# Every product matmul walks its columns in pieces of four, with a hop of 64 bytes, in four passes over the row

## The chip, the cores and the metric

The kernel runs on one core of one Trainium2 chip. The metric is the device time of one execution in microseconds (us). Before the change the median of three runs is 770.9 us (770.83 to 771.6).

## What is computed

The reference has one layer (`DEPTH = 1`), and that layer is the gated short-convolution mixer between two RMS norms. Batch is 1, there are 1024 rows (positions), the model width is 1024, the inner width 2048, and the convolution has 3 taps. All data is float32.

```python
def rms_norm(x, g):
    y = x * lax.rsqrt(jnp.mean(x * x, axis=-1, keepdims=True) + EPS)
    return y * g

def short_conv_mixer(u, w_in, conv_w, w_out):
    z, bg, cg, v = jnp.split(u @ w_in, 4, axis=-1)          # w_in: 1024 x 8192
    y = bg * causal_dwconv(cg * v, conv_w) * jax.nn.silu(z)
    return y @ w_out                                        # w_out: 2048 x 1024

u = rms_norm(x, pre_norm)
out = x + rms_norm(short_conv_mixer(u, sc_w_in, sc_conv_w, sc_w_out), post_norm)
```

## The kernel before

Nearly all of the work is two matrix products, and both run on TensorE (PE in the profile). A matmul instruction there holds a stationary operand of 128x128 weights and lets a moving operand of 128 partitions by 512 or 256 columns stream past it; the result, 128 partitions by the same columns, is added into a PSUM bank (512 float32 columns). Each matmul is preceded by its own weight load, which the profile lists as PEld.

**Three matmuls for one product.** The operands are float32, and the fast type on TensorE is float32r, which rounds. So every operand is split into a high part and a low part (`hi`, `lo` of the weights, `UH`, `UL` of the normed input), and a product is three matmuls into the same bank: `lo` x `UH`, `hi` x `UL`, `hi` x `UH`.

**Seven products for eight.** The input product is cut into 2x2 blocks (two halves of the contraction, two halves of 512 rows) and computed with seven block products in place of eight; they are called a to g. There are 16 channel blocks of 128 and two pairs of outputs for each (gate and value, then z and the other gate), so 32 pairs `p`. The banks are `px`, `py` and `pv`. Function `product` issues the twelve matmuls of one block product: four contraction tiles of 128 by three matmuls, 512 columns each. The first pair is computed by eight products (`plain`, banks `pp`). For most channel blocks the products b, f and g are cut once more in the same way: `deep_product` issues matmuls of 256 columns (banks with a 2 in the name, as `px2b`, and also `px`, `pv`). The output product is done in the same fashion by `out_mm` (512 columns, banks `po_x`, `po_v`) and `small_mm` (256 columns, banks `pb_`, `pf_`).

**Where the moving operand lies.** U stands in SBUF tiles of shape [128, 2, 4, 512] (high and low part, four contraction tiles, 512 rows), so the columns of one matmul are 512 or 256 neighbouring float32 in each partition. The output columns are neighbours in the bank as well. All start addresses of U's slices and of the output slices in the built program are multiples of 64 bytes.

**What sets the order.** All instructions are recorded first and then put in an order by a planner (class `Plan`), which knows the number of elements of an operand and which stretch of a tile it touches, but not the order in which an instruction walks it. TensorE's own order is the recorded order. The waits between engines are semaphores, set by the layer that emits the program. The names in the rows below are the program's tiles; a row says operation, out<-moving operand,weights and the shape.

Of the kernel before, what the change touches and what calls it, by code (L numbers as in the profile page):

```python
# [668 lines left out]
def kernel(  # L669
# [16 lines left out]
    nc = plan = Plan(tc.nc)  # L686
# [29 lines left out]
    def bank(name):  # L716
        return psum.tile([P, HB], F32, tag="bank", name=name)
# [136 lines left out]
    UH, UL = {}, {}  # L854
# [7 lines left out]

    banks = {}

    def product(p, i, ks=None):

        w = wt[p, i]
        which = {"b": "y", "e": "v", "f": "v"}.get(i, "x")
        first = i in "abe"
        if first and (p, which) not in banks:  # L870
            banks[p, which] = bank(f"p{which}_{p}")
        ps = banks[p, which]
        for k in range(KH) if ks is None else ks:
            hi, lo = (h[:, k * P : (k + 1) * P] for h in w)
            last = k == KH - 1
            nc.tensor.matmul(ps, lo, UH[i][:, k], start=first and k == 0, stop=False, skip_group_check=True)
            nc.tensor.matmul(ps, hi, UL[i][:, k], start=False, stop=False, skip_group_check=True)
            nc.tensor.matmul(ps, hi, UH[i][:, k], start=False, stop=last, skip_group_check=True)

    sn, cvs = {}, {}  # L880

# [235 lines left out]
    def plain(p, n, half, part, kks=range(4), first=None, last=None):  # L1117

        i = "abef"[2 * half + part]
        if (p, n, half) not in banks:  # L1120
            banks[p, n, half] = bank(f"pp_{p}_{n}_{half}")
        ps, w = banks[p, n, half], plain_w[p, n, part]
        first = part == 0 if first is None else first
        last = part == 1 if last is None else last
        for j, kk in enumerate(kks):
            hi, lo = (h[:, kk * P : (kk + 1) * P] for h in w)
            end = last and j == len(kks) - 1
            nc.tensor.matmul(ps, hi, UH[i][:, kk], start=first and j == 0, stop=False, skip_group_check=True)
            nc.tensor.matmul(ps, lo, UH[i][:, kk], start=False, stop=False, skip_group_check=True)
            nc.tensor.matmul(ps, hi, UL[i][:, kk], start=False, stop=end, skip_group_check=True)  # L1130

    def plain_snap(p, n):
        t = page(f"sp{n}_{p}")
# [69 lines left out]
    for k in range(KH):  # L1203
        plain(0, 0, 0, 0, [k], first=k == 0)
        for t in range(TH - 2 if k < KH - 1 else 0, TH):
            turn(k + KH, t)
# [5 lines left out]
    square_v(TH + 1)  # L1212
    plain_snap(0, 0)
    plain(0, 1, 0, 0)
    for k in (6, 7):
        read_k(k)
    high_plain(0, 1, [1])
    low_plain(0, 1, [1])
    plain_snap(0, 1)
    plain(0, 0, 0, 1)  # L1220
    plain(0, 1, 0, 1)
    rebuild([0])
# [45 lines left out]
    def plain_late(kk, part):  # L1268

        for n in (0, 1):  # L1270
            plain(0, n, 1, part, [kk], first=part == 1 and kk == 0, last=part == 0 and kk == KH - 1)

    product(1, "b", (0, 1))
    turn2(0)
    second(0)
    product(1, "b", (2, 3))
    sn[1, "a"] = page("sna_1")
    nc.scalar.copy(sn[1, "a"], banks[1, "y"])
    product(1, "a", (0, 1))
    turn2(1)  # L1280
    second(1)
# [105 lines left out]
    HH, KQ = HB // 2, KH // 2  # L1387
# [72 lines left out]
    def deep_product(z, c, i):  # L1460


        n, off = DEEP_W[i]
        if z == "f" and i in ("b'", "g'"):
            ps, first = banks[2 * c + (i == "g'"), "v"], False
        elif z == "g" and i in ("b'", "f'", "g'"):
            ps, first = banks[2 * c + (i == "g'"), "x"][:, HH if i == "f'" else 0 :], False
        else:
            which, first = z + DEEP_C[i][0], i in ("a'", "b'", "e'")
            if first:  # L1470
                banks[c, which] = bank(f"p{which[1]}2{z}_{c}")
            ps = banks[c, which]
        ps = ps[:, :HH]
        for k in range(KQ):
            hi, lo = (h[:, off + k * P : off + (k + 1) * P] for h in deep_w[z, c, n])
            if (z, i) in deep:
                uh, ul = (t[:, k] for t in deep[z, i])
            else:
                kk, l0 = {"a'": (k, 0), "b'": (k + KQ, 0), "e'": (k, HH), "f'": (k + KQ, HH)}[i]
                uh, ul = (u[z][:, kk, l0 : l0 + HH] for u in (UH, UL))  # L1480
            nc.tensor.matmul(ps, lo, uh, start=first and k == 0, stop=False, skip_group_check=True)
            nc.tensor.matmul(ps, hi, ul, start=False, stop=False, skip_group_check=True)
            nc.tensor.matmul(ps, hi, uh, start=False, stop=k == KQ - 1, skip_group_check=True)

    def deep_after(c, i):
        which, row, half = DEEP_C[i]
# [190 lines left out]
    for p in range(2, len(PAIRS)):  # L1677
        q, c = p + 1, p // 2
# [91 lines left out]
    for n, slot in enumerate(slots):  # L1770
        if slot[2:]:
            z, i, c = slot
            deep_product(z, c, i)
            if (i, c) == ("e'", LAST[z] - 1) and LAST[z] < NC:
                restore_u(z)

            early = (z, i) in (("f", "c'"), ("f", "e'"))
            if early:
                deep_after_f(c, i)
            if (z, i) != ("f", "c'"):  # L1780
                prepare(n)
            if z == "f":
                if not early:
                    deep_after_f(c, i)
                continue
            if z == "g":
                deep_after_g(c, i)
                if (i, c) == ("d'", NC - 1):
                    at_end("g")
                continue  # L1790
            deep_after(c, i)
            if (i, c) == ("f'", NC - 1):
                third_unit(0)
            elif i == "g'" and c == NC - 1:
                nc.scalar.activation(sn[2 * c + 1, "a"], sn[2 * c + 1, "a"], AF.Silu)
            continue
        i, p = slot
# [89 lines left out]
    def out_mm(i, h, q):  # L1887
        which = "v" if i == "e" else "x"
        if (which, q) not in ob:
            ob[which, q] = bank(f"po_{which}{q}")  # L1890
        ps, u, y = ob[which, q], OP["u", i, h], OP["y", i, h]
        for k in range(CQ):
            hi, lo = (y[:, z, k, q * P : (q + 1) * P] for z in (0, 1))
            first, last = i in "abe" and h == 0 and k == 0, h == 1 and k == CQ - 1
            nc.tensor.matmul(ps, lo, u[:, 0, k], start=first, stop=False, skip_group_check=True)
            nc.tensor.matmul(ps, hi, u[:, 1, k], start=False, stop=False, skip_group_check=True)
            nc.tensor.matmul(ps, hi, u[:, 0, k], start=False, stop=last, skip_group_check=True)

    def halves_of(t):
        q = t % TH  # L1900
# [79 lines left out]
    def small_mm(of_, i):  # L1980
        which = {"b'": "y'", "e'": "v'", "f'": "v'"}.get(i, "x'")
        first = i in ("a'", "b'", "e'")
        if first:
            ob[which] = bank(f"p{of_}_{which[0]}")
        if i in OUT_A:
            n, a0 = OUT_A[i]
            yh, yl = (small_op[of_, n][:, z, :, a0 : a0 + HH] for z in (0, 1))
        else:
            yh, yl = (small_op[of_, "X"][:, 0, z] for z in (0, 1))
        if i in OUT_B:  # L1990
            n, b0 = OUT_B[i]
            uh, ul = (small_op[of_, n][:, z, :, b0 : b0 + HH] for z in (0, 1))
        else:
            uh, ul = (small_op[of_, "X"][:, 1, z] for z in (0, 1))
        for j in (0, 1):
            ps = ob[which][:, j * HH : (j + 1) * HH]
            for k in range(CQ):
                hi, lo = (y[:, k, j * P : (j + 1) * P] for y in (yh, yl))

                start, stop = first and j == 0 and k == 0, k == CQ - 1  # L2000
                nc.tensor.matmul(ps, lo, uh[:, k], start=start, stop=False, skip_group_check=True)
                nc.tensor.matmul(ps, hi, ul[:, k], start=False, stop=False, skip_group_check=True)
                nc.tensor.matmul(ps, hi, uh[:, k], start=False, stop=stop, skip_group_check=True)

    def small_add(of_, i):
        which, row, half = DEEP_C[i]
# [68 lines left out]
    for i, h in OUT[:-2]:  # L2075
        if i in "bf":
            if h == 0:
                product_b() if i == "b" else product_f()
            continue
        for q in range(TH):  # L2080
            out_mm(i, h, q)
        BESIDE[i, h]()
        if h == 1:
            for q in range(TH):
                combine(i, q)
# [5 lines left out]
    for q in range(TH):  # L2091
        for h in (0, 1):
            out_mm("g", h, q)
        if q == TH - 1:
            plan.flush(PLAN)
        combine("g", q)
        finish_row(q + TH)
# [24 lines left out]
```

## Time and profile before

| | |
|---|---|
| median of three runs | 770.9 us (770.83 to 771.6) |
| span of the profiled execution, first to last instruction | 768.7 us |
| its own time outside the profiler | not given; the median stands 2.2 us above the span |
| TensorE busy (matmuls) | 758.4 us, 99% of the span, 4320 instructions |
| weight loads busy (beside the matmuls) | 665.9 us, 4320 instructions |
| VectorE (DVE) busy | 678.9 us, 1022 instructions |
| ScalarE (ACT) busy | 459.4 us, 880 instructions |
| GpSimd (POOL) busy | 464.1 us, 416 instructions |
| granted TensorE clock, mean | 0.998 |

How to read it: matmuls are pipelined, and the profile models the end of each, so a matmul's listed duration (390 ns for 512 columns) is longer than what it adds to the time. What it adds is the distance from its start to the start of the next one. Of the 4320 matmuls 102 are no products: 36 small ones that only keep the clock up (`pw`), 64 transposes of the input (`pk`) and two tiny transposes. The other 4218 are the products: 2244 of 512 columns and 1974 of 256.

### The profile page before, as it was taken

To read this page: it belongs to the slowest core of one execution; us is meant where nothing else is said; L and a number is where in the kernel's file an instruction comes from. 1 tells how busy PE (TensorE), PEld (TensorE's weight loads), DVE (VectorE), ACT (ScalarE), POOL (GpSimd) and SP (SyncE) were. 2 spreads that over 40 slices of the span, in tenths; PEclk is the share of its full clock that TensorE was granted. 3 is DMA by queue.
4 is the path that set the end of the run, shared out by engine and by line. 5 is a ranking of instruction groups with operands and counts; after the bars stand their busy time and mean duration, and the time that the engine had idled before them with its cause. 6 is when DMAs were issued, how large, how long until landed. Compare 5 with 4: busy or idle time off the path is not lost.

```text
span 768.7 us, 12791 instructions
## 1 busy us (share of the span) xinstructions
PE 758.4 (99%) x4320; PEld 665.9 (87%) x4320; DVE 678.9 (88%) x1022; ACT 459.4 (60%) x880; POOL 464.1 (60%) x416
## 2 busy tenths in 40 slices
PE   8999999999999999999999999999999999999996
PEld 6888888898989898988898898989888889889885
DVE  6899978999988979989999999898988898877993
ACT  7765678675656565556555665556553656564731
POOL 2509997889675778696789678584739100600421
PEclk9999999999999999999999999999999999999999
DMA  9213325243333547576859484928465998666842
GB/s 317 68 55 84 110 83 150 103 139 130 98 117 97 171 110 200 136 187 164 252 125 255 103 240 97 255 85 211 122 177 179 334 363 291 203 221 204 278 148 109
DMA packets 117137, 130.11 MB, mean 169 GB/s; under 512 B 7320, under 2 KB 74704, under 8 KB 116944
## 3 DMA queue, kind: packets, MB, share of 16 engines
q1 hardware_dynamic: 112560, 120.77, 49.3%
q0 software_dynamic: 4352, 8.39, 7.2%
q8 instruction: 34, 0.56, 0.3%
q14 instruction: 31, 0.25, 0.1%
q10 hardware_dynamic: 160, 0.14, 0.1%
HBM read 101.74 MB, written 44.30 MB: 190 GB/s over the span
## 4 chain that ended last, share of the span: by engine, by line
PE 97%; DVE 1%; DMA 1%; ACT 0%; POOL 0%; issue 0%; POOLq 0%; ACTq 0%
PE px L292 39%; PE pv L292 15%; PE po_x L292 11%; PE px2b L292 5%; PE px2f L292 4%; PE px2g L292 3%; PE po_v L292 3%; PE pp L292 3%; PE pv2b L292 3%; PE pv2f L292 2%; PE pf_x L292 1%; PE pb_x L292 1%; PE py2b L292 1%; PE py L292 1%; PE pv2g L292 1%; PE pb_v L292 1%
## 5 line engine op out<-in xcount | busy, mean ns | idle before, releaser
L292 PE MATMUL px<-u_a,wah 128*128 128x512 f32 x248 | 76.6, 390 | 0.0
L292 PE MATMUL px<-u_c,wch 128*128 128x512 f32 x248 | 76.5, 390 | 0.0
L292 PE MATMUL px<-u_d,wdh 128*128 128x512 f32 x248 | 76.4, 389 | 0.0
L292 PE MATMUL pv<-u_e,weh 128*128 128x512 f32 x248 | 76.3, 389 | 0.0
L292 ACT COPY beside<-raw 128x512 f32<-128x512 f32 x67 | 39.6, 591 | 31.1 <-DVE wal L292 10.4
L292 DVE SCALAR_TENSOR_TENSOR cv<-gpad,cw,cv 128x1024 f32<-128x1024 f32 x32 | 51.6, 1612 | 3.5 <-ACT cv L292 3.3
L292 PEld LDWEIGHTS px<-u_c,wch 128*128 128x128 f32 x248 | 46.5, 188 | 8.9
L292 PEld LDWEIGHTS px<-u_a,wah 128*128 128x128 f32 x248 | 46.6, 188 | 8.9
L292 PEld LDWEIGHTS pv<-u_e,weh 128*128 128x128 f32 x248 | 46.5, 188 | 8.7
L292 PEld LDWEIGHTS px<-u_d,wdh 128*128 128x128 f32 x248 | 46.6, 188 | 8.6
L292 POOL TENSOR_TENSOR sf<-raw,sc 128x512 f32<-128x512 f32 x30 | 47.2, 1573 | 9.5 <-DVE sc L292 7.1
L292 PE MATMUL px<-u_a,wal 128*128 128x512 f32 x124 | 48.4, 391 | 0.0
L292 PE MATMUL px<-u_c,wcl 128*128 128x512 f32 x124 | 48.4, 391 | 0.0
L292 PE MATMUL px<-u_d,wdl 128*128 128x512 f32 x124 | 48.4, 390 | 0.0
L292 PE MATMUL pv<-u_e,wel 128*128 128x512 f32 x124 | 48.2, 389 | 0.0
L292 POOL TENSOR_TENSOR rs_post<-ve_post,minus_half 128x1 f32<-128x1 f32 x7 | 6.5, 941 | 67.3 <-DVE ve_post L292 67.3
L292 POOL TENSOR_TENSOR sc<-se,raw 128x512 f32<-128x512 f32 x25 | 35.0, 1401 | 19.2 <-DVE se L292 10.2
L292 POOL TENSOR_TENSOR raw<-raw,raw 128x512 f32<-128x512 f32 x31 | 44.6, 1437 | 3.2 <-DVE se L292 2.9
L292 ACT COPY sna<-px 128x512 f32<-128x512 f32 x30 | 17.6, 586 | 45.4 <-PE px L292 45.1
L292 POOL TENSOR_TENSOR se<-raw,raw 128x512 f32<-128x512 f32 x22 | 32.8, 1491 | 18.1 <-DMA raw<-in_sc_w_in 11.3
L292 DVE TENSOR_TENSOR wcl<-sc,wch 128x512 fp32r<-128x512 f32 x31 | 31.7, 1023 | 2.8 <-ACT wch L292 2.8
L292 DVE TENSOR_TENSOR sna<-px2b,sna 128x256 f32<-128x256 f32 x56 | 23.2, 415 | 10.2 <-PE px2b L292 10.2
(486 smaller groups left out, 2637.3 us busy)
## 6 DMA issues: line engine op xcount, KB each, us to landing
raw<-in_sc_w_in SPq DMA_DIRECT2D x128, 256.0 KB, 4.7
y_d<-cv SPq DMA_DIRECT2D x16, 512.0 KB, 2.9
s_d<-s SPq DMA_DIRECT2D x32, 256.0 KB, 4.9
t_d<-in_sc_w_out POOLq DMA_DIRECT2D x16, 512.0 KB, 8.5
tb<-in_sc_w_out SPq DMA_DIRECT2D x16, 256.0 KB, 3.5
t_d<-in_sc_w_out SPq DMA_DIRECT2D x16, 256.0 KB, 4.6
t_d<-t_d SPq DMA_DIRECT2D x16, 256.0 KB, 4.5
s<-y_d SPq DMA_DIRECT2D x16, 256.0 KB, 4.6
```

Source lines behind the costliest of these rows:

```text
L292: getattr(engine, name)(*(self.plain(a) for a in args), **{k: self.plain(a) for k, a in kw.items()})
```

## The change

A helper `walk` gives the same columns in another order, and every product matmul uses it for the moving operand and for the output alike. A row of 512 columns is seen as 32 groups of 16 columns (64 bytes), each group as four pieces of four columns (16 bytes). The instruction takes the first piece of each group, hopping 64 bytes from piece to piece, then the second piece of each, and so on: four passes over the row. With 256 columns there are 16 groups. Each column still meets its own output column once, so the sums are the same. Weights, transposes and warm-up matmuls stay as they are.

```diff
+    def walk(a):
+        return a.rearrange("p (h c n) -> p c h n", c=4, n=4)
+
     def product(p, i, ks=None):
 ...
-            nc.tensor.matmul(ps, lo, UH[i][:, k], start=first and k == 0, stop=False, skip_group_check=True)
-            nc.tensor.matmul(ps, hi, UL[i][:, k], start=False, stop=False, skip_group_check=True)
-            nc.tensor.matmul(ps, hi, UH[i][:, k], start=False, stop=last, skip_group_check=True)
+            nc.tensor.matmul(walk(ps), lo, walk(UH[i][:, k]), start=first and k == 0, stop=False, skip_group_check=True)
+            nc.tensor.matmul(walk(ps), hi, walk(UL[i][:, k]), start=False, stop=False, skip_group_check=True)
+            nc.tensor.matmul(walk(ps), hi, walk(UH[i][:, k]), start=False, stop=last, skip_group_check=True)
 ...
     def out_mm(i, h, q):
 ...
-            nc.tensor.matmul(ps, lo, u[:, 0, k], start=first, stop=False, skip_group_check=True)
+            nc.tensor.matmul(walk(ps), lo, walk(u[:, 0, k]), start=first, stop=False, skip_group_check=True)
 ...
```

The same edit is made to all three matmuls in `plain`, `deep_product`, `out_mm` and `small_mm`.

The order of the instructions is the same on all five engines; only shapes and some waits differ. On TensorE, at the second product of a pair in the middle of the head (`px_668` and `pv_747` are banks, `u_c` and `u_e` moving operands, `wch`, `wcl`, `weh`, `wel` the high and low weights), this stood before:

```order
L292 MATMUL px_668<-u_c,wcl_692 128x512
L292 MATMUL px_668<-u_c,wch_685 128x512 x2
L292 MATMUL pv_747<-u_e,wel_702 128x512 [waits DVE_49]
L292 MATMUL pv_747<-u_e,weh_675 128x512 x2
L292 MATMUL pv_747<-u_e,wel_702 128x512
```

and now:

```order
L292 MATMUL px_668<-u_c,wcl_692 128x4x32x4
L292 MATMUL px_668<-u_c,wch_685 128x4x32x4 x2
L292 MATMUL pv_747<-u_e,wel_702 128x4x32x4 [waits DVE_49,PE_49]
L292 MATMUL pv_747<-u_e,weh_675 128x4x32x4 x2
L292 MATMUL pv_747<-u_e,wel_702 128x4x32x4
```

Nothing moved; the first matmul into a bank that was used before now also waits for TensorE's own semaphore, that is for the matmuls of the bank's earlier use. Such waits stand on 111 instructions of TensorE's queue in place of 62. One of the 62 that were there before, at the start of the pair ahead of that place on TensorE:

```order
L292 MATMUL px_417<-u_g,wgl_609 128x512
L292 MATMUL px_417<-u_g,wgh_608 128x512 x2
L292 MATMUL px_668<-u_a,wal_643 128x512 [waits DVE_49,PE_49]
L292 MATMUL px_668<-u_a,wah_642 128x512 [waits Activation_49]
L292 MATMUL px_668<-u_a,wah_642 128x512
```

This place stands in the new program unchanged but for the shapes.

More of the change, by code (lines that the diff above doesn't have):

```diff
@@ L1127, in plain @@
             end = last and j == len(kks) - 1
-            nc.tensor.matmul(ps, hi, UH[i][:, kk], start=first and j == 0, stop=False, skip_group_check=True)
-            nc.tensor.matmul(ps, lo, UH[i][:, kk], start=False, stop=False, skip_group_check=True)
-            nc.tensor.matmul(ps, hi, UL[i][:, kk], start=False, stop=end, skip_group_check=True)
+            nc.tensor.matmul(walk(ps), hi, walk(UH[i][:, kk]), start=first and j == 0, stop=False, skip_group_check=True)
+            nc.tensor.matmul(walk(ps), lo, walk(UH[i][:, kk]), start=False, stop=False, skip_group_check=True)
+            nc.tensor.matmul(walk(ps), hi, walk(UL[i][:, kk]), start=False, stop=end, skip_group_check=True)
     def plain_snap(p, n):
@@ L1480, in deep_product @@
                 uh, ul = (u[z][:, kk, l0 : l0 + HH] for u in (UH, UL))
-            nc.tensor.matmul(ps, lo, uh, start=first and k == 0, stop=False, skip_group_check=True)
-            nc.tensor.matmul(ps, hi, ul, start=False, stop=False, skip_group_check=True)
-            nc.tensor.matmul(ps, hi, uh, start=False, stop=k == KQ - 1, skip_group_check=True)
+            nc.tensor.matmul(walk(ps), lo, walk(uh), start=first and k == 0, stop=False, skip_group_check=True)
+            nc.tensor.matmul(walk(ps), hi, walk(ul), start=False, stop=False, skip_group_check=True)
+            nc.tensor.matmul(walk(ps), hi, walk(uh), start=False, stop=k == KQ - 1, skip_group_check=True)
     def deep_after(c, i):
@@ L1894, in out_mm @@
             first, last = i in "abe" and h == 0 and k == 0, h == 1 and k == CQ - 1
-            nc.tensor.matmul(ps, lo, u[:, 0, k], start=first, stop=False, skip_group_check=True)
-            nc.tensor.matmul(ps, hi, u[:, 1, k], start=False, stop=False, skip_group_check=True)
-            nc.tensor.matmul(ps, hi, u[:, 0, k], start=False, stop=last, skip_group_check=True)
+            nc.tensor.matmul(walk(ps), lo, walk(u[:, 0, k]), start=first, stop=False, skip_group_check=True)
+            nc.tensor.matmul(walk(ps), hi, walk(u[:, 1, k]), start=False, stop=False, skip_group_check=True)
+            nc.tensor.matmul(walk(ps), hi, walk(u[:, 0, k]), start=False, stop=last, skip_group_check=True)
     def halves_of(t):
@@ L2000, in small_mm @@
                 start, stop = first and j == 0 and k == 0, k == CQ - 1
-                nc.tensor.matmul(ps, lo, uh[:, k], start=start, stop=False, skip_group_check=True)
-                nc.tensor.matmul(ps, hi, ul[:, k], start=False, stop=False, skip_group_check=True)
-                nc.tensor.matmul(ps, hi, uh[:, k], start=False, stop=stop, skip_group_check=True)
+                nc.tensor.matmul(walk(ps), lo, walk(uh[:, k]), start=start, stop=False, skip_group_check=True)
+                nc.tensor.matmul(walk(ps), hi, walk(ul[:, k]), start=False, stop=False, skip_group_check=True)
+                nc.tensor.matmul(walk(ps), hi, walk(uh[:, k]), start=False, stop=stop, skip_group_check=True)
     def small_add(of_, i):
```

## The prediction

> **What bounds the kernel now.** I read the page's busy times first, then the chain that ended last, then the list of waits of TensorE, and last the timeline of TensorE, to get the distance between starts.
>
> ```profile
> span 768.7 us, 12791 instructions
> PE 758.4 (99%) x4320; PEld 665.9 (87%) x4320; DVE 678.9 (88%) x1022; ACT 459.4 (60%) x880; POOL 464.1 (60%) x416
> PEclk9999999999999999999999999999999999999999
> PE 97%; DVE 1%; DMA 1%; ACT 0%; POOL 0%; issue 0%; POOLq 0%; ACTq 0%
> ```
>
> The first row is the span, the second the busy time of each engine, the third the granted TensorE clock in 40 slices (at least nine tenths everywhere), the fourth the chain of waits that ended last. TensorE holds 97% of that chain. It is not late for anything but its own stream:
>
> ```profile
> PE pk L292 <- DVE ve_pre L292: 1.5, 1, 1.5
> PE pw L292 <- DVE idle L292: 1.1, 1, 1.1
> PE pp L292 <- ACT u_a L292: 0.5, 1, 0.5
> PE pk L292 <- DVE xa L292: 0.4, 1, 0.4
> ```
>
> These are all of TensorE's waits in the whole span: 3.5 us, all in the head. So what one product matmul takes, from its start to the next one's start, is the kernel's time. The next rows (start, length, what, count) give it, first for 256 columns and then for 512:
>
> ```profile
> 703.80 2.99 PE L292 MATMUL pf_x<-oB_f,oA_f 128*128 128x256 f32 x24
> 706.63 3.03 PE L292 MATMUL pf_v<-oB_f,oA_f 128*128 128x256 f32 x24
> 709.49 3.03 PE L292 MATMUL pf_x<-oB_f,oA_f 128*128 128x256 f32 x24
> 712.36 2.90 PE L292 MATMUL pf_v<-oB_f,ox_f 128*128 128x256 f32 x24
> 715.10 3.02 PE L292 MATMUL pf_x<-ox_f,oA_f 128*128 128x256 f32 x24
> 717.97 22.00 PE L292 MATMUL po_x<-ou_d,oy_d 128*128 128x512 f32 x96
> 739.80 22.14 PE L292 MATMUL po_x<-ou_g,oy_g 128*128 128x512 f32 x96
> ```
>
> From 703.80 to 717.97 there are five groups of 24, so 14.17 us / 120 = 118.1 ns for a matmul of 256 columns. From 717.97 to 739.80 there are 96, so 21.83 / 96 = 227.4 ns for 512. The 256 further columns cost 109.3 ns: 0.427 ns a column, and 227.4 - 512 x 0.427 = 8.8 ns a matmul whatever its width. The whole stream is 2244 x 227.4 + 1974 x 118.1 ns = 510.3 + 233.1 = 743.4 us, of which the columns (1,654,272 of them) are 706.4 us. The first product starts here:
>
> ```profile
> 12.61 0.50 PE L292 MATMUL pp<-u_a,wn00h 128*128 128x512 f32 x1 [0.45 <-ACT u_a L292]
> ```
>
> With 12.6 us ahead of it and 768.7 - (739.80 + 21.83) = 7.1 us behind the last one the sum is 763.1 us; the other 5.6 us of the span are the transposes that lie between products and the slower products of the head. The span is that of one profiled execution, whose own time is not given; the median of 770.9 us is 2.2 us more, and I take those 2.2 us as lying around the span and unchanged.
>
> **The change, part by part.**
>
> *The order of the columns.* The count of matmuls, columns, weights and weight loads is what it was. What can change is the 0.427 ns of a column and the 8.8 ns of a matmul. Since no wait of TensorE is left behind the head, nothing covers a change of either: the other engines follow, and a slower TensorE only gives them room (VectorE, the next, is busy 678.9 us). The trace has no matmul that walks with hops, so the price is bounded from neighbours. The nearest rows are those where ScalarE and VectorE read operands with and without hops. `u_c` is made from `xb` in eight pieces of 128 columns that lie 1024 columns apart (two contraction tiles by four row tiles); `u_d` is made from `xa`, without hops:
>
> ```profile
> L292 ACT CAST u_c<-xb 128x1024 fp32r<-128x1024 f32 x2 | 2.0, 1042 | 0.0
> L292 ACT CAST u_d<-xa 128x1024 fp32r<-128x1024 f32 x2 | 2.1, 1050 | 2.2 <-DVE xa L292 2.1
> L292 DVE TENSOR_TENSOR u_c<-xb,u_c 128x1024 fp32r<-128x1024 f32 x2 | 2.4, 1222 | 0.0
> L292 DVE TENSOR_TENSOR u_d<-xa,u_d 128x1024 fp32r<-128x1024 f32 x2 | 2.4, 1220 | 0.0
> ```
>
> The mean of one (the second number behind the bar) is 1042 ns with hops and 1050 without on ScalarE, 1222 and 1220 on VectorE. Two nanoseconds over eight pieces is at most 0.25 ns a hop, and the other engine gives less than nothing. So the lower end is no cost. A gain is excluded, but for a small chance, because the array takes the same columns and the 8.8 ns are the same at both widths, so they belong to the change of instruction and not to the walk. The upper end is far: a hop could cost a TensorE piece as long as its four columns take, 1.7 ns. I take zero: it is what the two rows say of the address walk, and a piece of four columns still brings four neighbours of 16 bytes on an aligned address, in U and in the bank. Two weaknesses of that reading stay and make the range: those rows have pieces of 128 columns and not of four, and TensorE takes a column in 0.427 ns where VectorE, by those rows, needs 1222 / 1024 = 1.19 ns.
>
> [...]
>
> *The new waits.* 49 more instructions of TensorE's queue wait for TensorE's own semaphore, most on the first matmul into a bank used before, as on `pv_747`. In the program's order the awaited matmul stands at least 43 matmuls ahead on every one of the 49 (43 x 118 ns = 5.1 us), so none has to wait; 19 of the waits are instructions of their own that only wait, of which the queue had 107. Behind the waiting matmul on that queue stand all later products, so a wait that did cost would be paid in full. One that was there before, on `px_668`, shows its price:
>
> ```profile
> 58.86 0.63 PE L292 MATMUL px<-u_g,wgh 128*128 128x512 f32 x2
> 59.32 0.39 PE L292 MATMUL px<-u_a,wal 128*128 128x512 f32 x1
> 59.55 0.63 PE L292 MATMUL px<-u_a,wah 128*128 128x512 f32 x2
> ```
>
> The waiting matmul starts at 59.32, 0.46 us after the first of the two ahead of it, so 0.23 us a matmul, and the next starts 0.23 us later. The price is 0, at most the 0.01 us to which the rows are rounded: 49 x 0.01 = 0.5 us. One more wait of that kind stands on VectorE in the tail, for the last products; the operation already follows ScalarE's square of the same bank, which itself follows those products, so it is late for nothing.
>
> Sum: 770.9 + 0 + 0 = 770.9 us, same as before. A measurement of this kernel tells about 0.2% from no change (1.5 us, so 769.4 to 772.4).
>
> **The rivals.**
>
> *A cost for each pass or each matmul.* Where the walk goes back to the start of the row, three times in a matmul, the reader could lose time. If it loses one piece (4 x 0.427 = 1.7 ns), that is 4218 x 3 x 1.7 = 21.6 us, 792 us in all; if it loses as much as a change of instruction does (8.8 ns), 4218 x 3 x 8.8 = 111 us, 882 us. For it speaks that each matmul has fixed nanoseconds already; against it, that ScalarE and VectorE go back in the same way between tiles in `u_c` and show nothing. Chance 0.07.
>
> *A cost for each piece.* Every hop costs one column's time: 413,568 pieces x 0.427 ns = 177 us, 947 us. For it speaks that TensorE reads faster than any engine whose hops the trace shows; against it the 0.25 ns bound of VectorE, which would give at most 103 us. Chance 0.08.
>
> *The memory behind the walk halves the rate.* A piece costs as much again as its four columns, because the bank or U delivers neighbours ahead only when the row is walked through: 706.4 us more, 1477 us. It decides as soon as a piece takes longer to reach than the 1.7 ns in which the array eats one; below that it costs nothing. For it speaks that the stream has no slack at all (0.427 ns a column over the whole span), against it that the piece is aligned and whole. [...] Chance 0.11.
>
> *Faster.* Only if the 8.8 ns shrank, for instance because a matmul returns to the columns of the one before it in another rhythm: 1 ns less would be 4.2 us, 767 us. No row speaks for it. Chance 0.02.
>
> **How the numbers follow.** No change has 0.72, the three slower cases together 0.26, faster 0.02. The predicted time is that of no change, 770.9 us. The range begins at 768, which takes in half of the faster case, and must reach into the slower ones: with the cost per pass up to its bound of 882 us it holds 0.72 + 0.07 + 0.01 = 0.80, so it ends there. The likeliest case alone has 769.4 to 772.4.
>
> **What the profile of the changed kernel would show.** If I am right: 118 and 227 ns between starts of the `pf_` and `po_x` groups, TensorE busy near 758 us, the `px_668` place with 0.23 us between starts, and no new row in TensorE's waits. A cost per pass would raise both distances by the same nanoseconds; a cost per piece would raise the 512-column one by twice what it adds to the 256-column one. If a wait cost something, the distances inside a group would stand and only first matmuls of a bank would start late. What would make the prediction wrong is above all a memory that serves a 64-byte hop more slowly than the next piece, which no row before can show.

## Result: 762.6 us in place of 770.9, a ratio of 0.989, and the profile after

The changed kernel takes 762.61 us (median of 4 runs, 762.2 to 763.14) beside 770.87 us for the kernel before on the same chip (4 runs, 770.09 to 771.6). The ratio is 0.9893 with a 95% interval of 0.9879 to 0.9907. So the change makes the kernel faster by 1.1%, where no change was forecast. The profiled execution took 762.5 us with a span of 760.7 us.

The page of the changed kernel: span, busy times, granted clock, and the chain of waits that ended last.

```profile
span 760.7 us, 12810 instructions
PE 750.5 (99%) x4320; PEld 662.0 (87%) x4320; DVE 679.1 (89%) x1022; ACT 458.8 (60%) x880; POOL 462.1 (61%) x416
PEclk9999999999999999999999999999999999999999
PE 86%; DVE 6%; POOL 2%; DMA 2%; ACT 2%; issue 1%; POOLq 0%; DVEq 0%; SPq 0%; ACTq 0%
```

TensorE is busy 7.9 us less (758.4 before), the span is 8.0 us shorter, the clock is the same (0.998), and VectorE's busy time is the same to 0.2 us. The same work of TensorE takes less time. TensorE now holds 86% of the chain that ended last, in place of 97%.

The timeline of TensorE in the tail, the same groups as before (start, length, what, count):

```profile
696.66 2.94 PE L292 MATMUL pf_x<-oB_f,oA_f 128*128 128x256 f32 x24
699.44 2.95 PE L292 MATMUL pf_v<-oB_f,oA_f 128*128 128x256 f32 x24
702.22 2.88 PE L292 MATMUL pf_x<-oB_f,oA_f 128*128 128x256 f32 x24
704.94 2.91 PE L292 MATMUL pf_v<-oB_f,ox_f 128*128 128x256 f32 x24
707.69 2.88 PE L292 MATMUL pf_x<-ox_f,oA_f 128*128 128x256 f32 x24
710.41 21.79 PE L292 MATMUL po_x<-ou_d,oy_d 128*128 128x512 f32 x96
732.04 21.94 PE L292 MATMUL po_x<-ou_g,oy_g 128*128 128x512 f32 x96
```

From 696.66 to 710.41 there are 120 matmuls: 13.75 / 120 = 114.6 ns for 256 columns (118.1 before). From 710.41 to 732.04 there are 96: 21.63 / 96 = 225.3 ns for 512 (227.4 before). Over the whole span, with the starts of all products read from the trace and the late ones left out, the mean distance goes from 227.7 to 225.6 ns for 512 columns and from 117.7 to 114.7 ns for 256.

The tile view of `u_g` shows how the gain is spread. It gives the shortest, the median and the longest duration in ns of one group. Before:

```profile
L292 PE MATMUL px<-u_g,dwg0h x48: 281/281/281, 129.8 to 533.2; 128*128 128x256 f32 x48
L292 PE MATMUL px2g<-u_g,dwg0h x48: 281/281/281, 130.5 to 533.9; 128*128 128x256 f32 x48
```

and after:

```profile
L292 PE MATMUL px<-u_g,dwg0h x48: 270/276/280, 128.0 to 527.6; 128*128 128x256 f32 x48
L292 PE MATMUL px2g<-u_g,dwg0h x48: 271/277/312, 128.7 to 528.3; 128*128 128x256 f32 x48
```

Before, all 48 take the same 281 ns, in 400 us of the span. After, they take 270 to 280. The ends of matmuls are modelled, so the starts are the safer measure: from the start of each of the 48 `px` matmuls to the next start it is 117 to 119 ns before and 109 to 120 after. A fixed cost of an instruction would not be expected to start to vary; something that depends on how two streams happen to lie in time would.

The list of waits of TensorE after (waiting tile, releaser, us in total, times, longest):

```profile
PE pw L292 <- DVE idle L292: 1.1, 1, 1.1
PE px L292 <- DVE u_g L292: 0.5, 1, 0.5
PE px2b L292 <- DVE dwb1l L292: 0.5, 1, 0.5
PE pp L292 <- ACT u_a L292: 0.5, 1, 0.5
PE pk L292 <- DVE xa L292: 0.3, 1, 0.3
PE pv2f L292 <- DVE dwf2l L292: 0.2, 1, 0.2
PE px L292 <- DVE wcl L292: 0.2, 1, 0.2
```

There are four new rows behind the head: TensorE now waits for weights that VectorE makes (`dwb1l`, `dwf2l`, `wcl`), and once for VectorE at `u_g`, 1.4 us in all. It has become fast enough to arrive there early. By the distances the products should gain 2244 x 2.1 + 1974 x 3.0 ns = 4.7 + 5.9 = 10.6 us. From the start of the first product to the start of the last the trace has 748.9 us before and 741.1 after, 7.8 us less; the starts that come late behind the head add up to 2.6 us more than before (the largest at 403, 412, 550 and 737 us; the first three stand in the list of waits, the last does not). 10.6 - 2.6 is 8.0 us, the change of the span.

The place at `px_668` once more, with its wait, from the timeline after:

```profile
57.99 0.61 PE L292 MATMUL px<-u_g,wgh 128*128 128x512 f32 x2
58.44 0.38 PE L292 MATMUL px<-u_a,wal 128*128 128x512 f32 x1
58.66 0.61 PE L292 MATMUL px<-u_a,wah 128*128 128x512 f32 x2
```

The waiting matmul starts 0.45 us after the first of the two ahead of it and the next follows after 0.22 us: no gap.

### The profile page after: what moved, and what is told of

Its sections match the earlier page's. It is cut to its first block, busy times and chain, and to the rows that moved or that the text cites. A ratio compares the mean times of both kernels' runs of the same rounds, so it can differ in the third digit from the quotient of the medians.

```text
span 760.7 us, 12810 instructions
## 1 busy us (share of the span) xinstructions
PE 750.5 (99%) x4320; PEld 662.0 (87%) x4320; DVE 679.1 (89%) x1022; ACT 458.8 (60%) x880; POOL 462.1 (61%) x416
## 3 DMA queue, kind: packets, MB, share of 16 engines
q1 hardware_dynamic: 112560, 120.77, 49.8%
## 4 chain that ended last, share of the span: by engine, by line
PE 86%; DVE 6%; POOL 2%; DMA 2%; ACT 2%; issue 1%; POOLq 0%; DVEq 0%; SPq 0%; ACTq 0%
PE px L292 36%; PE pv L292 14%; PE po_x L292 8%; PE px2b L292 5%; PE px2f L292 3%; PE px2g L292 3%; PE po_v L292 3%; PE pp L292 3%; PE pv2b L292 2%; PE pv2f L292 2%; PE pb_x L292 1%; PE py2b L292 1%; PE py L292 1%; DMA raw<-in_sc_w_in 1%; PE pv2g L292 1%
## 5 line engine op out<-in xcount | busy, mean ns | idle before, releaser
L292 ACT COPY beside<-raw 128x512 f32<-128x512 f32 x67 | 39.6, 591 | 33.1 <-DVE wal L292 10.6
L292 DVE SCALAR_TENSOR_TENSOR cv<-gpad,cw,cv 128x1024 f32<-128x1024 f32 x32 | 49.9, 1560 | 3.3 <-ACT cv L292 3.2
L292 POOL TENSOR_TENSOR sne<-snc,sne 128x512 f32<-128x512 f32 x12 | 17.9, 1489 | 23.8 <-ACT snc L292 23.8
```

The source lines that it names most:

```text
L292: getattr(engine, name)(*(self.plain(a) for a in args), **{k: self.plain(a) for k, a in kw.items()})
```

## Experiments

The questions, in the order in which they were asked: is the gain on the side of U or of the bank; does it need this walk or only any pattern of more dimensions; if it is U's side, what does U's reading collide with; and which hops and pieces gain. The experiments are told by question, not by time. "512 and 256 distance" is always the mean from one product's start to the next one's of the same width, for the input products from 30 us on, worked out from the starts in the trace. It leaves out only distances over twice the usual one, so some late starts are still in it; in the kernel before it is 227.9 and 117.7 ns, after the change 226.3 and 114.8.

### U's side or the bank's

**U alone is walked**, the bank is written in a row.

```diff
-            nc.tensor.matmul(walk(ps), lo, walk(UH[i][:, k]), ...
+            nc.tensor.matmul(ps, lo, walk(UH[i][:, k]), ...
```

> Only the moving operand U is walked in pieces of four; the bank is written in plain order, so the result's columns stand in another order (the kernel's output is not the reference's). Distances between starts before: 227.4 ns at 512 columns (po_x groups) and 118.1 ns at 256 (pf groups); with the whole change 225.3 and 114.6. Theory A (the plain walk of U collides with the weight load that reads SBUF beside it, and the hops break that up): the whole gain is here, 225.3 and 114.6 ns, about 762.6 us. Theory B (the gain is on the side of the bank, where the walk changes how sums are read and written back): 227.4 and 118.1 ns, 771 us. Theory C (any pattern of more than one dimension makes the change from one matmul to the next shorter): a part or all of the gain.

Measured: 762.6 us (759.9 to 765.85), ratio 0.9894, interval 0.9864 to 0.9923. Its timeline of TensorE in the tail:

```profile
697.04 2.94 PE L292 MATMUL pf_x<-oB_f,oA_f 128*128 128x256 f32 x24
...
710.79 21.79 PE L292 MATMUL po_x<-ou_d,oy_d 128*128 128x512 f32 x96
732.41 21.60 PE L292 MATMUL po_x<-ou_g,oy_g 128*128 128x512 f32 x96
```

13.75 / 120 = 114.6 ns and 21.62 / 96 = 225.2 ns, as with the whole change. The gain is on U's side, all of it.

**The bank alone is walked.** This kernel also has 48 of the 49 new waits of the change (110 instructions wait for TensorE's own semaphore, 111 in the change), which U alone does not bring (62).

```diff
-            nc.tensor.matmul(walk(ps), lo, walk(UH[i][:, k]), ...
+            nc.tensor.matmul(walk(ps), lo, UH[i][:, k], ...
```

> Only the bank is walked in pieces of four; U is read in plain order (the output's columns stand in another order). The 49 new waits are in. Theory A: 227.4 and 118.1 ns, 771 us. Theory B: 225.3 and 114.6 ns, 762.6 us. Theory C: part or all of the gain.

Measured: 771.14 us, ratio 1.0005 (0.9996 to 1.0015). The timeline:

```profile
704.86 2.99 PE L292 MATMUL pf_x<-oB_f,oA_f 128*128 128x256 f32 x24
...
719.02 22.00 PE L292 MATMUL po_x<-ou_d,oy_d 128*128 128x512 f32 x96
740.85 22.14 PE L292 MATMUL po_x<-ou_g,oy_g 128*128 128x512 f32 x96
```

14.16 / 120 = 118.0 ns and 21.83 / 96 = 227.4 ns, those of the kernel before. The order in which a bank is written and the new waits together neither cost nor gain anything here (771.14 us beside 771.01 for the kernel before on the same chip).

### The walk or the form of the pattern

**Long pieces**: the same number of dimensions in the pattern, but 64 columns in a row before the hop of 512 bytes, for U and the bank.

```diff
-        return a.rearrange("p (h c n) -> p c h n", c=4, n=4)
+        return a.rearrange("p (h c n) -> p c h n", c=2, n=64)
```

> U and bank walked in pieces of 64 columns (256 bytes) with a hop of 512 bytes, two passes; the result is the reference's. The pattern has as many dimensions as in the change, but inside a piece the columns run as before. Theory A: close to before, 226 to 228 and 117 to 118 ns, about 770 us, since the plain walk is broken only every 64 columns. Theory B: the same. Theory C: the whole gain, 225.3 and 114.6 ns, 762.6 us.

Measured: 770.83 us, ratio 1.0001 (0.9991 to 1.001). A pattern of three dimensions gained nothing by itself here; the order of addresses did (762.61 us).

**Pieces of 8 columns**, the hop still 64 bytes, two passes.

```diff
+        return a.rearrange("p (h c n) -> p c h n", c=2, n=8)
```

> U and bank walked in pieces of eight columns (32 bytes) with a hop of 64 bytes, two passes; the result is the reference's. Theory A: between before and the change, 226.3 and 116.3 ns, about 766.5 us, since half as many places of each 64 bytes are hopped over. Theory B: between too. Theory C: the whole gain, 762.6 us.

Measured: 782.01 us, ratio 1.0148 (1.0131 to 1.0165): slower, against the expectations. Its timeline:

```profile
728.62 22.52 PE L292 MATMUL po_x<-ou_d,oy_d 128*128 128x512 f32 x96
750.98 22.56 PE L292 MATMUL po_x<-ou_g,oy_g 128*128 128x512 f32 x96
```

22.36 / 96 = 232.9 ns. So a walk is not always a help. For the `po_x` matmuls the distance falls from 227.4 to 225.3 ns with pieces of four and rises to 232.9 with pieces of eight. A cost that can fall or rise with the order speaks, to the author, for a collision and against a saved latency.

### What U's reading collides with

While one matmul reads U, the weights of the next are loaded (in the kernel before the loads are busy for 665.9 us beside 758.4 us of matmuls); both lie in SBUF tiles. In the kernel before, the matmuls can be sorted by how far the next weights lie from U in the low address bits (the addresses of the built program, modulo 256 bytes, with the starts of the trace from 30 us on, those over 25 ns late left out). Where they lie at the same place, which is so for 1771 of them, 512 columns take 227.3 ns; 64 bytes apart (72 of them) 231.8; 192 apart (219) 229.0. The 72 have their weights at the same place modulo 256 as most of the 1771, so the place of the weights alone does not make the difference. If the distance is cause and not company, moving the weights alone must move the time.

**The weights moved by 32 bytes** in the kernel before, nothing walked. A gap is put behind the second group of U's tiles, so that the tiles behind it, which hold most weights of the input products, lie 32 bytes later. U's own tiles and the output products' operands are not moved; the sums of U's blocks that part of the 256-column products read (tiles `u..._deep`) lie behind the gap too and move with their weights.

```diff
 U_LAYOUT = (
     ((0, 3, 4), 64),
-    ((1, 2, 5, 6), 0),
+    ((1, 2, 5, 6), 32),
 )
```

> The kernel before, with 32 bytes left free ahead of the tiles that hold most weights of the input product, so that they lie 32 bytes further against U than before; nothing else is changed. Theory A1 (U's plain reads collide with the weight load beside them, by the low bits of the two addresses): the distances of the input products leave 227 and 118 ns by 1 to 4 ns, either way, and the time moves by 3 to 12 us. Theory A2 (the time between two matmuls belongs to how U is read alone, for instance to the start of a stream): 227 and 118 ns, 771 us.

Measured: 778.29 us, ratio 1.0092 (1.0077 to 1.0107). First the kernel before, timeline of TensorE in the middle, then this one (a step from `wcl` to `wcl` is three matmuls, and there are two steps between the rows shown):

```profile
299.53 0.39 PE L292 MATMUL px<-u_c,wcl 128*128 128x512 f32 x1
...
300.89 0.39 PE L292 MATMUL px<-u_c,wcl 128*128 128x512 f32 x1
```

```profile
303.64 0.40 PE L292 MATMUL px<-u_c,wcl 128*128 128x512 f32 x1
...
305.03 0.40 PE L292 MATMUL px<-u_c,wcl 128*128 128x512 f32 x1
...
711.62 2.99 PE L292 MATMUL pf_x<-oB_f,oA_f 128*128 128x256 f32 x24
...
725.78 21.99 PE L292 MATMUL po_x<-ou_d,oy_d 128*128 128x512 f32 x96
747.61 22.14 PE L292 MATMUL po_x<-ou_g,oy_g 128*128 128x512 f32 x96
```

Six matmuls take 1.36 us before and 1.39 with the shift, 227 and 232 ns each. Over all input products the 512 distance is 232.7 in place of 227.9, the 256 distance 117.4 in place of 117.7. The output products, in the same kernel on the same engine, keep their 14.16 / 120 = 118.0 and 21.83 / 96 = 227.4 ns. An address alone, with no instruction changed, makes 4.8 ns a matmul of 512 columns. For 256 columns the mean hides two groups, which are told apart behind the next run.

**The weights moved by 64 bytes**, to see whether the distance of 64 is as dear as the sorting of the kernel before says.

```diff
+    ((1, 2, 5, 6), 64),
```

> The kernel before (plain walk) with 64 bytes left free ahead of the tiles with most weights of the input product. 32 bytes gave 778.3 us. If only the distance of the low address bits counts, the products at 512 columns come to the 232 ns that the few products at that distance have in the kernel before, and the time to 776 to 781 us; if a shift alone can do what the walk does, 760 to 765 us; if 64 bytes is a whole period, 771 us.

Measured: 779.2 us, ratio 1.0102 (1.0085 to 1.0119); 512 distance 233.4 ns, where the sorting gave 231.8.

At 256 columns the two shifts did two things. For 850 of these matmuls only the next weights moved: their distance between starts went from 117.7 ns to 118.1 (32 bytes) and 118.7 (64 bytes). The other 674 read the `u..._deep` tiles, which moved by as much as their weights: from 117.7 to 116.4 and 115.7, with weights and moving operand as far apart as before. So the address counts at 256 columns as well, the means (117.4 with the shift of 32 bytes) are the net of a loss and a gain, and the distance between the two operands is not all that counts.

**The changed kernel with the weights moved by 32 bytes**, to see whether the walk depends on the address too.

```diff
     ((0, 3, 4), 64),
-    ((1, 2, 5, 6), 0),
+    ((1, 2, 5, 6), 32),
```

> The changed kernel (pieces of four, hop of 64 bytes) with the same 32 bytes free ahead of the weights. Theory A1: the distances of the input products (mean 227 and 115 ns there, spread over 217 to 234 and 109 to 124) change their mean by 1 ns or more; the time moves from 762.6 by 3 us or more, either way. Theory A2: 762.6 us.

Measured: 763.84 us, ratio 0.9907 to the kernel before (0.989 to 0.9924). The 512 distance goes from 226.3 to 227.2, the 256 distance from 114.8 to 115.0. What cost 7.3 us without the walk (778.29 - 771.04) costs 1.2 us with it (763.84 - 762.61), and the runs of the two kernels overlap (762.61 to 765.47, 762.2 to 763.14). This missed what was expected of a collision (3 us or more). That the walk breaks a lockstep, a fixed rhythm in which the two streams meet, and so hardly cares about the address, is the author's account, given after this run and shown by none; the stepped load below, beside which the walk gains 8.3 ns at 512 columns, agrees with it.

**The weight load walks, U does not.** In the kernel before, the weight load of the input products takes every second column of 256 (the count of loads and columns stays, the columns of the weights are mixed, so the result is another); the output products load as before. The loads in `deep_product` get the same step.

```diff
-            hi, lo = (h[:, k * P : (k + 1) * P] for h in w)
+            hi, lo = (h[:, k // 2 * 2 * P + k % 2 : (k // 2 + 1) * 2 * P : 2] for h in w)
```

> The kernel before with plain U and bank; in the input products of seven blocks each weight load takes every second column of a stretch of 256 instead of 128 neighbours (64 places of 16 bytes instead of 32; the columns of the weights are mixed, so the output is not the reference's). U is read as before. If the weight load is what U's reads collide with, the distances of those products leave 227 and 118 ns by several ns (twice the places to collide at: up to 9 ns more, 4000 x 9 ns = up to 36 us), while the output products keep 227.4 and 118.1 ns. If the weight load is not the partner: 771 us and all distances as before. If the stepped load itself becomes longer than a matmul of 256 columns, its own length in the profile leaves 188 ns.

Measured: 782.32 us, ratio 1.0148 (1.0131 to 1.0165). Groups of the weight loads (behind the bar busy us, mean ns of one, idle us) and then the output products of its timeline:

```profile
L292 PEld LDWEIGHTS px<-u_c,wch 128*128 128x128 f32 x248 | 47.9, 193 | 8.8
L292 PEld LDWEIGHTS po_x<-ou_g,oy_g 128*128 128x128 f32 x96 | 18.0, 188 | 3.9
```

```profile
729.72 22.00 PE L292 MATMUL po_x<-ou_d,oy_d 128*128 128x512 f32 x96
751.55 22.14 PE L292 MATMUL po_x<-ou_g,oy_g 128*128 128x512 f32 x96
```

The load itself becomes 5 ns longer (193 beside 188), and the matmul beside it too: 233.0 ns for 512 columns, 119.7 for 256, while the output products stay at 21.83 / 96 = 227.4. A load of 193 ns would fit beside a matmul of 228 ns, so by its length it should not slow the 512 ones, and no tile moved in this run. So how the weights are loaded changes the time of the matmul beside the load, and this is shown for 512 columns (233.0 ns beside 227.9). At 256 columns the load (193 ns) is longer than the distance between two matmuls (119.7), so there a longer load could set the pace by itself, and this run does not tell that from a collision.

**Both walk**: the changed kernel with the stepped weight load.

> The same stepped weight loads in the changed kernel (pieces of four, hop of 64 bytes; output not the reference's). If the weight load is the partner, the input products leave their means of 226.5 and 114.8 ns too, and the output products keep 225.3 and 114.6. If not: 762.6 us.

Measured: 765.72 us, ratio 0.9932 (0.9912 to 0.9952). Its weight loads:

```profile
L292 PEld LDWEIGHTS px<-u_c,wch 128*128 128x128 f32 x248 | 48.6, 196 | 6.3
```

The 512 distance is 224.7, the lowest of all input products measured, 8.3 ns under the same load without the walk, though the load now takes 196 ns; so at 512 columns the load's length does not set the pace. The 256 distance is 119.3: there the walk hardly helps (119.7 without it).

With no instruction added, the two shifts and the stepped load moved the time of a matmul of 512 columns by up to 5.5 ns (233.4 beside 227.9) with where, and in which step, the weights were read.

### Which pieces and hops

**Pairs of columns**, hop 64 bytes, eight passes, for U and the bank; then the same for U alone and for the bank alone.

```diff
+        return a.rearrange("p (h c n) -> p c h n", c=8, n=2)
```

> U and bank walked in pieces of two columns (8 bytes) with a hop of 64 bytes, eight passes. A piece is then half of 16 bytes of U and one pair of neighbours in the bank. [...] Theory A1 says only that the fixed part changes by some nanoseconds either way.

> Pieces of two columns with a hop of 64 bytes in U alone; the bank in plain order (the output's columns stand in another order). The same walk on both took 1432 us, 431 and 218 to 228 ns. If U's side sets that (a fetch of 16 bytes of U takes as long as four columns, 1.67 ns, however many of them are used): 1432 us again. If the bank's side sets it: 760 to 785 us.

> Pieces of two columns with a hop of 64 bytes in the bank alone; U in plain order (the output's columns stand in another order). If U's side sets the cost of pairs: 227.4 and 118.1 ns, 771 us. If the bank's side: 1432 us.

Measured: 1432.1 us for both (ratio 1.8574, 1.8547 to 1.8602), 1432.06 for U alone (1.8576, 1.8539 to 1.8613), 771.02 for the bank alone (1.0003, 0.9993 to 1.0014). The busy times of the three pages, in that order:

```profile
PE 1421.3 (99%) x4320; PEld 884.5 (62%) x4320; DVE 637.8 (45%) x1022; ACT 463.8 (32%) x880; POOL 411.1 (29%) x416
```

```profile
PE 1419.9 (99%) x4320; PEld 883.1 (62%) x4320; DVE 638.0 (45%) x1022; ACT 462.7 (32%) x880; POOL 409.0 (29%) x416
```

```profile
PE 760.3 (99%) x4320; PEld 667.1 (87%) x4320; DVE 678.2 (88%) x1022; ACT 459.2 (60%) x880; POOL 463.0 (60%) x416
```

The distances with pairs are 431.8 and 222.1 ns, so (431.8 - 222.1) / 256 = 0.82 ns a column or 1.64 ns a pair. In the plain walk four columns take 4 x 0.427 = 1.71 ns. So a pair of columns with a hop of 64 bytes costs about what four columns in a row cost. That is the halved rate that the prediction priced at 1477 us; it is there with pieces of 8 bytes (1432.1 us), not with pieces of 16 at the same hop (762.61), and only in U. A bank took pairs for nothing (771.02 us), as it took pieces of four (771.14).

**Other hops with pieces of four columns**: 32, 128 and 256 bytes, and 256 bytes for U alone.

```diff
+        return a.rearrange("p (h c n) -> p c h n", c=2, n=4)     # hop 32 bytes
+        return a.rearrange("p (h c n) -> p c h n", c=8, n=4)     # hop 128 bytes
+        return a.rearrange("p (h c n) -> p c h n", c=16, n=4)    # hop 256 bytes
```

> Pieces of four columns with a hop of 32 bytes in U and bank, two passes. Nothing below a piece is torn, so the columns keep 0.42 ns; only the fixed part against the weight load changes. Collision theory: between 217 and 236, and 109 and 122 ns, 750 to 785 us; if a hop keeps the columns' reads off part of the lines of the weight load, hop 32 does half of what hop 64 does, 767 us.

> Pieces of four columns with a hop of 128 bytes, eight passes. Hop 64 took 762.6 us and hop 256 took 919. If the cost at 256 bytes grows step by step, 128 lies between: 780 to 860 us; if it comes only when all pieces of a pass meet the same place of a memory that repeats every 256 bytes, 128 bytes is free of it: 755 to 775 us.

> U and bank walked in pieces of four columns with a hop of 256 bytes, sixteen passes. Theory A1: the fixed part changes again, since other low address bits move with the pieces: not 225.3 and 114.6 ns; between 216 and 236 and between 109 and 125. Theory A2: as in the change, 762.6 us, since the start of the stream is broken in the same way.

> Pieces of four with a hop of 256 bytes in U alone, the bank in plain order (the output's columns stand in another order). With the walk on both 919 us, 278 and 136 ns. If U's reads meet the same part of SBUF again and again: 919 us. If the bank's side pays it: 755 to 785 us.

**Longer pieces with a hop of 128 bytes**: 16 columns in two passes, 8 columns in four.

```diff
+        return a.rearrange("p (h c n) -> p c h n", c=2, n=16)
+        return a.rearrange("p (h c n) -> p c h n", c=4, n=8)
```

> U and bank in pieces of 16 columns (64 bytes) with a hop of 128 bytes, two passes. Pieces of 64 columns with a hop of 512 bytes kept 771 us, pieces of 8 with a hop of 64 took 782, pieces of 4 with a hop of 128 took 824. If what counts is how many of the 16-byte places of a 256-byte period a pass touches (8 of 16 here, as with a hop of 32 bytes, 781 us): 776 to 786 us. If long pieces read as plain: 771 us.

> U and bank in pieces of eight columns (32 bytes) with a hop of 128 bytes, four passes. If what counts is how many of the 16-byte places of a 256-byte period a pass touches (4 of 16 here, as with the change): 758 to 768 us. If what counts is the hop: near the 824 us of the hop of 128 bytes with pieces of four, or between it and 782.

Measured, all of them in one table:

| piece, hop | us | ratio, interval | 512 and 256 distance, ns |
|---|---|---|---|
| 4 columns, 32 bytes | 780.92 | 1.013 (1.0115 to 1.0145) | 231.9, 118.3 |
| 4 columns, 64 bytes (the change) | 762.61 | 0.9893 (0.9879 to 0.9907) | 226.3, 114.8 |
| 4 columns, 128 bytes | 824.2 | 1.069 (1.0672 to 1.0708) | 245.9, 125.0 |
| 4 columns, 256 bytes | 918.81 | 1.1915 (1.1895 to 1.1935) | 277.7, 136.5 |
| the same, U alone | 918.98 | 1.1915 (1.1891 to 1.1939) | 277.7, 136.5 |
| 8 columns, 64 bytes | 782.01 | 1.0148 (1.0131 to 1.0165) | 232.4, 118.3 |
| 8 columns, 128 bytes | 773.84 | 1.0031 (1.002 to 1.0043) | 229.5, 118.8 |
| 16 columns, 128 bytes | 804.64 | 1.0433 (1.0417 to 1.0448) | 240.6, 121.0 |
| 64 columns, 512 bytes | 770.83 | 1.0001 (0.9991 to 1.001) | as before |

The timeline of the kernel with a hop of 128 bytes, as an example of where the cost lies:

```profile
754.34 3.14 PE L292 MATMUL pf_x<-oB_f,oA_f 128*128 128x256 f32 x24
...
769.09 23.81 PE L292 MATMUL po_x<-ou_d,oy_d 128*128 128x512 f32 x96
792.73 23.21 PE L292 MATMUL po_x<-ou_g,oy_g 128*128 128x512 f32 x96
```

14.75 / 120 = 122.9 ns and 23.64 / 96 = 246.3 ns, 4.8 and 18.9 more than before: no fixed sum for a matmul, it grows with the columns, and with a hop of 256 bytes more so (18.8 and 49.8). The expectations for pieces of 8 with a hop of 64, for pieces of 4 with a hop of 256 (distances of 216 to 236 ns or no change from the walk) and for pieces of 16 and of 8 with a hop of 128 were missed, and a hop of 32 did not do half of what 64 does, so no rule that was put to a test stands behind the table. What it does show is that only one of these walks is faster than none.

No version tried is faster than the change itself; U alone is its equal within the interval.

## Why the prediction was wrong

**Right.** TensorE's stream is the bound: of the 10.6 us that the products gained 8.0 came out in the span, and 2.6 went into late starts, of which the list of waits puts 1.4 down to VectorE. The new waits cost nothing (771.14 us with 48 of the 49 and the bank walked). The walk of the bank costs nothing. The cover was rightly said to be missing: nothing hides a change of either distance.

**The step that failed** is the sentence "A gain is excluded, but for a small chance, because the array takes the same columns and the 8.8 ns are the same at both widths, so they belong to the change of instruction and not to the walk." It has two faults. The split into 0.427 ns a column and 8.8 ns a matmul was drawn through two widths, and two points always fit a line; that they fit says nothing about what the remainder is. And the remainder was not fixed: with the weights 32 bytes further on a matmul took 4.8 ns more at 512 columns and 0.4 more at 256 (where only the weights moved), with the stepped load 5.1 and 2.0 more, with the walk 2.1 and 3.0 less. So the nanoseconds that were booked as fixed belong at least in part to where and in which order U is read, and at 512 columns to the next weight load beside it. The trace of before had a hint that was not looked for: the matmuls sorted by the distance of their two addresses, 227.3 ns beside 231.8, are two groups with the same instruction and the same width.

**The price of the walk** was bounded by ScalarE's and VectorE's rows with hops (`u_c`, `u_d`). They gave zero, and for the bank it was zero. For U they were the wrong neighbours: by those rows ScalarE needs 1042 / 1024 = 1.02 ns a column and VectorE 1.19, and neither loads weights. No row of theirs could show a sum of the size of 2 to 3 ns a matmul, nor its sign. The other ground for zero, that a piece is four neighbours on an aligned address, was shown by no run before; with such pieces the kernel took from 762.61 to 918.81 us, by the hop.

**The rivals.** What happened is the one called faster, at 0.02, and by its own words (the remainder shrank because the columns come in another rhythm); its 1 ns was sized too small, 2.1 and 3.0 ns were measured. A cost for each pass did not show: pieces of 64 columns go back once for nothing (770.83 us). A rate nearly halved exists, for pairs in U (1432 us); that neighbours delivered ahead are behind it is not shown. A cost that grows with the columns, and so with the pieces, exists for hops of 128 and 256 bytes (824 and 919 us), though the number of pieces is the same as at 64. So the slower rivals were something real, which this hop and this piece avoid.

**What was to be seen.** Of the marks set for being right, the one without a gap at `px_668` came true (0.22 us from start to start); 118 and 227 ns did not (114.6 and 225.3), nor TensorE busy near 758 us (750.5), nor a list of waits without new rows.

**What stays open.** Why a hop of 64 bytes gains and 32, 128 and 256 lose. Why the walk of 256 columns gains 3.0 ns, which is over half of the whole gain (5.9 of 10.6 us): that this gain is U's side is shown, that the weight load has a part in it is not shown, and moving weights and moving operand together changed these matmuls by up to 2.0 ns. The distance of the two addresses does not explain 512 columns in full either: in the kernel before, 117 input products lie at the same place as their next weights, with U 64 bytes past a multiple of 256, and take 229.8 ns. And how much of a matmul's remainder is left to gain.

## What to carry to other kernels

When TensorE's stream is the bound and each matmul has some nanoseconds more than its columns explain, do not book them as an instruction's fixed cost: sort the matmuls by the low address bits of U and of the next weights, and move one of the two by 32 or 64 bytes. That is a change of one number, and here it moved the time by as much (7 to 8 us) as the walk, but both times to the slow side: most matmuls of 512 columns in the kernel before already lay at the best of the three distances tried. The one group that gained by a shift is that of the 256-column products whose two operands moved together. Of a walk of the moving operand, measure the piece and the hop: with a hop of 64 bytes pieces of 16 bytes took 762.61 us, pieces of 32 bytes 782.01 and pieces of 8 bytes 1432.1, and of the hops tried with pieces of 16 bytes only 64 bytes gained. The order in which a PSUM bank is written cost nothing here down to pairs of float32 (771.02 us).

## What the hardware showed that was not expected

- How U and the next weights lie, and how these are loaded, changes a matmul's time: the same instructions took 227.9 or 232.7 ns (512 columns) by a shift of 32 bytes, and a load stepped by two cost the matmul beside it 5.1 ns.
- In U a pair of columns with a hop of 64 bytes costs 1.64 ns and four columns in a row 1.71 ns (estimates from the distances with pairs and with the plain walk), so pairs nearly double the kernel's time (1432 us), while pieces of four at the same hop do not (762.6 us).
- In the kernel before, the listed durations of 48 matmuls are the same to the nanosecond (281/281/281) and their starts 117 to 119 ns apart; walked, the starts are 109 to 120 ns apart, with a lower mean.
- Writing a bank in pieces of four or two columns cost nothing (771.14 and 771.02 us).
